# Differential attention: the product of weights and values for two query tiles at a time, in three float32r passes, with its norm and output moved a tile apart

## The chip, the cores and the metric

One core of one Trainium2 chip runs the whole program. The metric is the device time of one execution in microseconds (us). TensorE (PE) multiplies matrices and turns tiles, VectorE (DVE) and ScalarE (ACT) read its results from PSUM, GpSimd (POOL) does small element-wise work, and SyncE (SP) issues the DMAs.

## The reference

The program is a two-layer encoder trunk for 1024 tokens of width 1024. Layer 0 mixes tokens by neighbourhood attention, layer 1 by dense differential attention; each layer ends with a gated convolutional channel mixer and a gated embedding. The change concerns layer 1's mixer: 8 heads, each with two score maps of 64 channels and values of 128 channels.

```python
def diff_attention(h, w_qkv, lam, subln_g, w_o, t5_table, lambda_init):
    ...
    def block_fn(args):            # one block of 128 queries
        ...
        s = jnp.einsum('bhmqd,bhmkd->bhmqk', qb, k).astype(jnp.float32) + bias[None, :, None]
        a = jax.nn.softmax(s, axis=-1)
        w = a[:, :, 0] - lam_full * a[:, :, 1]
        return jnp.einsum('bhqk,bhkd->bhqd', w.astype(v.dtype), v)
    ...
    o = rms_norm(o, subln_g) * (1.0 - lambda_init)
    o = o.transpose(0, 2, 1, 3).reshape(B, S, D)
    return o @ w_o
```

## The kernel before, in words

All matrices are float32. Large products run in float32r, in three passes: an operand is split into a high part (a copy rounded to float32r, `high`, L134, on ACT) and a low part (what the copy left over, `low`, L137, a subtraction on DVE that reads the high part), and `mm3` (L169) adds high x high, high x low and low x high. `split` (L140) is the two together.

The mixer of layer 1 is `da` (L667). It works on chunks: chunk n is one head (n // 8) and one tile of 128 queries (n % 8), 64 chunks in all. For each chunk TensorE does this:

- `da_scores` (L591): both score maps of 128 queries x 1024 keys, 12 matmuls of 64 rows x 512 columns, into four PSUM banks. DVE then adds the bias and finds the row extreme of each map (L441), ACT takes the exponentials and their sums (L445), and DVE combines the two maps to the weights w (L616).
- `da_turn` (L619), twice: half g of the weights, four blocks of 128 x 128, is turned in one bank and copied to `wT`, half 0 by ACT (L631), half 1 by DVE (L633).
- `da_values` (L635): eight plain float32 matmuls, the turned weights as the stationary operand, 128 columns of values moving; the result is query x value. ACT squares and sums it (L645), POOL takes the root (L184), DVE scales (L648). The bank stays in use.
- `da_out` (L651): one transpose of the normed tile into the same bank, then ACT copies it out (L664; L661 in the last head) and SP stores it.

Beside the chunks runs a generator, `qkv_stream`: the projections of queries, keys and values of the next head in 48 steps of three matmuls (L172 to L174), their splits, the weights' loads and splits, and at the end the projected embeddings and the first part of the output product. `tick(part)` (L403) lets it go on by 6 x part steps, carrying fractions over; `need` runs it until a head's operands are there; `drain` runs the rest. The values of the next head are turned through the same two banks (L203) and copied by ACT (L372).

TensorE runs in the order in which the program is written. The order of the other engines is fixed ahead of the run by a planner with a model of times of its own, which in general puts the instruction that is earlier in the program first. Splits of late loads are put in a list of jobs and hung behind the softmax and the half 1 copy of the chunks (`job`, L747).

PSUM has eight banks: four for scores, two for the projections (pool `pj`), two for everything else here (pool `tr`, `bank()`, L126), handed out in turn. The four pages of pool `r2` (16 KB a partition) hold queries and keys of the heads in turn, and afterwards the embedding operands.

Of the kernel before, what the change touches and what calls it, by code (L numbers as in the profile page):

```python
# [8 lines left out]
F32 = mybir.dt.float32  # L9
F32R = mybir.dt.float32r  # L10
AF = mybir.ActivationFunctionType
ALU = mybir.AluOpType
# [4 lines left out]
P = 128  # L17
D = 1024
SEQ = 1024
NT = SEQ // P  # L20
KT = D // P
# [5 lines left out]
D_HEADS = 8  # L27
FT = 22
PK = 2
EPS = 1e-6  # L30
# [61 lines left out]
class Trunk:  # L92
# [88 lines left out]
        return self.root(ss)  # L181

    def root(self, ss):
        self.nc.gpsimd.tensor_tensor(out=ss, in0=ss, in1=self.mhalf, op=ALU.pow)  # L184
        return ss

    def normed(self, x, h, g=None, tag="ss"):
# [30 lines left out]
    def constants(self):  # L218
        nc, c = self.nc, self.const
        self.ident = c.tile([P, P], F32, tag="ident", name="ident")  # L220
        nc.sync.dma_start(self.ident, self.i["c_ident"])

        self.mhalf = c.tile([P, 1], F32, tag="mhalf", name="mhalf")
        nc.vector.memset(self.mhalf, -0.5)

    def late_constants(self):
# [69 lines left out]
    def qkv_stream(self, layer, hT, x, first, mid):  # L296


        nc = self.nc
# [2 lines left out]
        own = [slice(0, 64), slice(64, 128)]  # L302
        values = lambda: None
        for j in range(KT):
            A = self.page(self.r2, "r2", (P, 4, SEQ), F32R)
            if layer == 0:
                B = self.page(self.r2, "r2", (P, 4, SEQ), F32R)
                Q, KH, KL = [A[:, 0], A[:, 1]], [A[:, 2], A[:, 3]], [B[:, 0], B[:, 1]]
# [53 lines left out]
            if layer == 0:  # L362
                v = B[:, 2:4].rearrange("p a (t m w) -> p (a t) m w", t=4, m=2)

                def put(g, t):
                    o, t = v[:, 4 * g : 4 * g + 4], t.rearrange("p k (m w) -> p k m w", m=2)
                    self.split(t, o[:, :, :, 0:64], o[:, :, :, 64:128])
            else:
                v = self.page(x, "v", (P, KT, P))

                def put(g, t):
                    nc.scalar.activation(v[:, 4 * g : 4 * g + 4], t, AF.Copy)  # L372

            vT = self.page(self.raw, "raw")
            for tb in range(2):
# [58 lines left out]
            nc.gpsimd.tensor_tensor(out=v(B), in0=v(self.mask), in1=s, op=ALU.subtract)  # L434
        return B

    def softmax_pre(self, s, bias, e):

        nc = self.nc
        mn = self.col("mn")  # L440
        nc.vector.tensor_tensor_reduce(  # L441
            out=e, in0=s, in1=bias, scale=1.0, scalar=3e38, op0=ALU.add, op1=ALU.min, accum_out=mn
        )
        sm = self.col("sum")
        self.exp = nc.scalar.activation(e, e, AF.Exp, bias=mn, scale=-1.0, accum_out=sm).ins  # L445
        return sm

# [143 lines left out]
    def da_scores(self, x, n):  # L591

        nc = self.nc
        h, t = n // NT, n % NT
        A = self.qk[h]
        if t == 0:
            self.T = self.page(x, "T", (P, TW))
            nc.sync.dma_start(self.T, self.skewed[h][:, P - 1 : P - 1 + TW])
        s = [self.ps.tile([P, 1024], F32, tag="s", name=self.uid("s")) for _ in range(2)]
        q = slice(t * P, t * P + P)  # L600
        for half in range(2):
            w = slice(half * 512, half * 512 + 512)
            for z, (a, b) in enumerate(((0, 2), (0, 3), (1, 2))):
                for m in range(2):
                    o = slice(64 * m, 64 * m + 64)
                    nc.tensor.matmul(s[m][:, w], A[o, a, q], A[o, b, w], start=z == 0, stop=z == 2)  # L606
        a = (NT - 1 - t) * P
        e = [self.page(x, f"E{m}") for m in range(2)]
        r0, sm = [self.softmax_pre(s[m], self.T[:, a : a + SEQ], e[m]) for m in range(2)]
        w = e[0]  # L610
        self.chunk[n] = w, r0
        c = self.col("c")
        nc.vector.reciprocal(c, sm)
        nc.vector.scalar_tensor_tensor(out=c, in0=r0, scalar=c, in1=self.neglam, op0=ALU.mult, op1=ALU.mult)
        nc.vector.reciprocal(r0, r0)
        done = nc.vector.scalar_tensor_tensor(out=w, in0=e[1], scalar=c, in1=w, op0=ALU.mult, op1=ALU.add).ins  # L616
        self.job(self.exp, done)

    def da_turn(self, x, n, g):  # L619
        nc = self.nc  # L620
        w, r0 = self.chunk[n][:2]
        if g == 0:
            self.chunk[n] = w, r0, self.page(x, "wT", (P, KT, P))
        wT = self.chunk[n][2]
        t = self.bank()
        for k in range(4):
            c = (4 * g + k) * P
            nc.tensor.transpose(t[:, k * P : k * P + P], w[:, c : c + P], self.ident)  # L628
        t = t.rearrange("p (k t) -> p k t", k=4)
        if g == 0:  # L630
            self.turned_w = nc.scalar.activation(wT[:, 0:4], t, AF.Copy).ins  # L631
        else:
            self.job(self.turned_w, nc.vector.tensor_copy(wT[:, 4:8], t).ins)  # L633

    def da_values(self, x, n):  # L635
        nc = self.nc
        V = self.v[2 * (n // NT)]
        _, r0, wT = self.chunk[n]
        b = self.bank()
        o = b[:, :P]  # L640
        for k in range(KT):
            nc.tensor.matmul(o, wT[:, k], V[:, k], start=k == 0, stop=k == KT - 1)  # L642
        os = self.page(x, "os", (P, P))
        r = self.col("ss")
        nc.scalar.activation(os, o, AF.Square, scale=r0, accum_out=r)  # L645
        nc.vector.tensor_scalar(out=r, in0=r, scalar1=1.0 / P, scalar2=EPS, op0=ALU.mult, op1=ALU.add)  # L646
        self.root(r)
        nc.vector.tensor_scalar(out=os, in0=o, scalar1=r0, scalar2=r, op0=ALU.mult, op1=ALU.mult)  # L648
        self.chunk[n] = b, os

    def da_out(self, x, n, oT):  # L651
        nc = self.nc
        h, t = n // NT, n % NT
        b, os = self.chunk.pop(n)
        tr = b[:, P : 2 * P]
        nc.tensor.transpose(tr, os, self.ident)
        cols = slice(t * P, t * P + P)
        if h == D_HEADS - 1:
            if t == 0:
                self.opage = self.page(self.raw, "raw")  # L660
            nc.scalar.activation(self.opage[:, cols], tr, AF.Copy, scale=self.subg)  # L661
        else:
            ot = self.page(x, "ot", (P, P))
            nc.scalar.activation(ot, tr, AF.Copy, scale=self.subg)  # L664
            nc.sync.dma_start(oT[h][:, cols], ot)

    def da(self, hT, oT, first, mid):  # L667

        N = NT * D_HEADS
        with self.tc.tile_pool(name="xa1", bufs=2, reuse_waits="tile") as x, \  # L670
             self.psum("s", 2) as self.ps:
            self.begin(self.qkv_stream(1, hT, x, first, mid))
            self.chunk = {}
            self.need(self.qk, 0)
            self.tick(6 / 6)
            self.da_scores(x, 0)
            self.tick(6 / 6)
            for n in range(N + 1):
                if n > 0:
                    self.need(self.v, (n - 1) // NT * 2 + 1)  # L680
                    self.da_values(x, n - 1)
                if n + 1 < N:
                    self.need(self.qk, (n + 1) // NT)
                    self.da_scores(x, n + 1)
                if n < N:
                    self.da_turn(x, n, 0)
                self.tick(0.34)
                if n < N:
                    self.da_turn(x, n, 1)
                self.tick(0.16)  # L690
                if n > 0:
                    self.da_out(x, n - 1, oT)
                self.tick(0.5)
            self.drain()

    def psum(self, name, bufs):
        return self.tc.tile_pool(name=self.uid("ps" + name), bufs=bufs, space=PSUM, reuse_waits="tile")
# [741 lines left out]

    def embeddings(self, layer):  # L1440

        nc = self.nc
        a = self.page(self.r2, "r2", (P, 2, 2, SEQ), F32R)
        b = self.page(self.r2, "r2", (P, 2, 2, D), F32R)
        load = []
        for k in range(2):
            rows = slice(k * P, k * P + P)
            for o, src in ((a, self.i["pT"]), (b, self.i["ple_w_proj"])):
                load.append((src[layer][rows], o[:, k, 0], o[:, k, 1]))
        if layer == 0:  # L1450
            for src, *parts in load:
                self.load_split(src, dst=parts)
        else:
            left = list(load)

            def begin(src, *parts):
                raw = self.page(self.raw, "raw")
                nc.sync.dma_start(raw, src)
                return raw, parts

            next_one = [begin(*left.pop(0))]

            def job():
                raw, parts = next_one.pop()
                did = self.split(raw, *parts)
                if left:
                    next_one.append(begin(*left.pop(0)))
                return did

            self.jobs += [job] * 4  # L1470
        yield
        while layer == 1 and next_one:
# [139 lines left out]
```

## Time and profile before

| | |
|---|---|
| median of 3 runs | 2758.91 us (2757.64 to 2758.96) |
| profiled execution | 2758.85 us, span 2757.1 us |
| PE, PEld (weight loads) | 2693.7 us (98%), 2225.7 us (81%) |
| DVE, ACT, POOL | 1938.5 us (70%), 1321.2 us (48%), 463.2 us (17%) |
| mean granted clock | 0.993 |
| stage of the change | from the first scores at 1348.9 us to the last output near 1928 us |

Busy time counts an instruction from start to end; matmuls overlap, so two starts in a row tell what one costs. The granted clock is given as a share of full speed: 1.00 is 2.4 GHz, 0.50 is 1.2 GHz.

### The profile page before, as it was taken

What the parts mean: (1) busy time and instruction counts of PE and PEld (TensorE: products, weight loads), DVE (VectorE), ACT (ScalarE), POOL (GpSimd) and SP (SyncE); (2) the same over time, 40 slices, a digit from 0 to 9 for tenths busy, and PEclk for the clock granted to TensorE, in tenths of its full rate; (3) what the DMA queues carried; (4) which work ended last, traced back from release to release, by engine and by line L of the source; (5) the groups of instructions that cost most, each with busy time, mean ns of one, the idle gap of its engine ahead of it and who ended that gap; (6) DMA issues with size and microseconds to landing.
All of it is one profiled execution on the core that took longest, in us unless ns stands there. A gap on an engine that the chain in (4) does not pass through costs nothing.

```text
span 2757.1 us, 36537 instructions
## 1 busy us (share of the span) xinstructions
PE 2693.7 (98%) x13440; PEld 2225.7 (81%) x13440; DVE 1938.5 (70%) x3317; ACT 1321.2 (48%) x2467; POOL 463.2 (17%) x461
## 2 busy tenths in 40 slices
PE   7999998999999999999999999999999999999998
PEld 5788887877888888888788888887887888888887
DVE  5677776579777777676566666676688777776664
ACT  4555556454444445454355555555454434444452
POOL 2121220004333310001000000000105333300000
PEclk9999999999999999999999999999999999999999
DMA  6512214533322373343211111123413323272342
GB/s 183 169 55 68 66 48 156 142 92 107 115 102 94 115 263 125 105 150 111 99 46 46 45 46 46 53 77 126 134 62 122 115 92 115 98 284 96 115 146 103
DMA packets 129476, 298.48 MB, mean 108 GB/s; under 512 B 11753, under 2 KB 37737, under 8 KB 129297
## 3 DMA queue, kind: packets, MB, share of 16 engines
q1 hardware_dynamic: 129296, 296.15, 32.5%
q8 instruction: 105, 1.72, 0.3%
q14 instruction: 75, 0.61, 0.1%
HBM read 221.69 MB, written 86.61 MB: 112 GB/s over the span
## 4 chain that ended last, share of the span: by engine, by line
PE 85%; DVE 6%; DMA 4%; ACT 2%; issue 2%; POOL 0%; SPq 0%; ACTq 0%; POOLq 0%; DVEq 0%
PE b L172 19%; PE b L173 19%; PE b L174 19%; PE g L770 6%; PE m L770 5%; PE b L642 4%; PE s L606 3%; PE b L628 2%; PE b L203 2%; PE av L512 1%; PE b L485 1%; DVE r L138 1%; PE b L770 1%; DMA raw<-in_qkv 1%; DMA x<-in_x 1%
## 5 line engine op out<-in xcount | busy, mean ns | idle before, releaser
L172 PE MATMUL b<-r,ws 128*128 128x512 f32 (+1 forms) x1328 | 547.3, 412 | 6.9 <-ACT ws L135 3.7
L173 PE MATMUL b<-r,ws 128*128 128x512 f32 (+1 forms) x1328 | 519.7, 391 | 1.4 <-DVE r L138 1.2
L174 PE MATMUL b<-r,ws 128*128 128x512 f32 (+1 forms) x1328 | 519.1, 391 | 0.5 <-DVE ws L138 0.5
L172 PEld LDWEIGHTS b<-r,ws 128*128 128x128 f32 x1328 | 252.8, 190 | 55.2 <-ACT ws L135 4.1
L174 PEld LDWEIGHTS b<-r,ws 128*128 128x128 f32 x1328 | 252.1, 190 | 54.8 <-DVE ws L138 1.0
L173 PEld LDWEIGHTS b<-r,ws 128*128 128x128 f32 x1328 | 253.3, 191 | 38.6 <-DVE r L138 3.5
L172 PE MATMUL b<-r,r 128*128 128x512 f32 x680 | 270.4, 398 | 9.5 <-ACT r L135 5.2
L184 POOL TENSOR_TENSOR ss<-ss,mhalf 128x1 f32<-128x1 f32 x136 | 84.0, 619 | 1142.1 <-DVE ss L646 563.3
L172 PE MATMUL b<-r,wa 128*128 128x512 f32 x688 | 269.0, 391 | 4.5 <-DVE B L1140 3.7
L445 ACT ACTIVATE E<-E,mn 128x1024 f32<-128x1024 f32 (+2 forms) x256 | 221.4, 866 | 105.2 <-DVE mn L441 104.7
L174 PE MATMUL b<-r,wa 128*128 128x512 f32 x688 | 268.6, 390 | 0.0
L173 PE MATMUL b<-r,wa 128*128 128x512 f32 x688 | 268.4, 390 | 0.0
L174 PE MATMUL b<-r,r 128*128 128x512 f32 x680 | 266.5, 392 | 1.0 <-DVE r L138 1.0
L173 PE MATMUL b<-r,r 128*128 128x512 f32 x680 | 266.8, 392 | 0.5 <-DVE r L138 0.5
L138 DVE TENSOR_TENSOR ws<-raw,ws 128x512 fp32r<-128x512 f32 (+3 forms) x168 | 171.1, 1026 | 61.1 <-ACT ws L135 58.6
L138 DVE TENSOR_TENSOR r<-raw,r 128x512 fp32r<-128x512 f32 (+1 forms) x170 | 129.1, 766 | 113.1 <-ACT r L135 110.0
L135 ACT ACTIVATE r<-raw 128x512 fp32r<-128x512 f32 (+1 forms) x170 | 112.7, 670 | 193.2 <-PE b L173 162.6
L135 ACT ACTIVATE ws<-raw 128x512 fp32r<-128x512 f32 (+3 forms) x168 | 124.3, 748 | 137.4 <-PE b L174 52.1
L172 PEld LDWEIGHTS b<-r,r 128*128 128x128 f32 x680 | 128.6, 189 | 38.6 <-ACT ws L1483 6.3
L770 PE MATMUL m<-r,ws 128*128 128x512 f32 x672 | 156.9, 393 | 0.0
L172 PEld LDWEIGHTS b<-r,wa 128*128 128x128 f32 x688 | 129.4, 188 | 33.5 <-DVE B L1140 5.2
L770 PE MATMUL g<-r,ws 128*128 128x512 f32 x672 | 155.8, 391 | 0.0
(178 smaller groups left out, 5110.4 us busy)
## 6 DMA issues: line engine op xcount, KB each, us to landing
raw<-in_w_in SPq DMA_DIRECT2D x86, 512.0 KB, 3.5
raw<-in_qkv SPq DMA_DIRECT2D x48, 512.0 KB, 5.6
spillS<-r SPq DMA_DIRECT2D x88, 256.0 KB, 3.2
r<-in_ffn_w_out SPq DMA_DIRECT2D x40, 512.0 KB, 10.1
raw<-spillS SPq DMA_DIRECT2D x40, 512.0 KB, 3.5
spillA<-B SPq DMA_DIRECT2D x66, 256.0 KB, 2.9
raw<-spillA SPq DMA_DIRECT2D x30, 512.0 KB, 4.0
x<-x SPq DMA_DIRECT2D x24, 512.0 KB, 3.7
```

Of the source, the lines that this page charges most:

```text
L135: return self.nc.scalar.activation(hi, src, AF.Copy).ins
L138: return self.nc.vector.tensor_tensor(out=lo, in0=src, in1=hi.bitcast(F32), op=ALU.subtract).ins
L172: mm(out, sta[0], mov[0], start=first, stop=False, skip_group_check=onto)
L173: mm(out, sta[0], mov[1], start=False, stop=False, skip_group_check=onto)
L174: mm(out, sta[1], mov[0], start=False, stop=last, skip_group_check=onto)
L184: self.nc.gpsimd.tensor_tensor(out=ss, in0=ss, in1=self.mhalf, op=ALU.pow)
L203: self.nc.tensor.transpose(t[:, k * P : k * P + P], h[:, c : c + P], self.ident)
L445: self.exp = nc.scalar.activation(e, e, AF.Exp, bias=mn, scale=-1.0, accum_out=sm).ins
L606: nc.tensor.matmul(s[m][:, w], A[o, a, q], A[o, b, w], start=z == 0, stop=z == 2)
L628: nc.tensor.transpose(t[:, k * P : k * P + P], w[:, c : c + P], self.ident)
L642: nc.tensor.matmul(o, wT[:, k], V[:, k], start=k == 0, stop=k == KT - 1)
L770: mm(out[half], a, b[:, w], start=first and k + z == 0, stop=last and k == n - 1 and z == 2)
```

## The change

Weights and values are multiplied for two chunks at a time, after the second of them, with the values stationary and 2 x 128 query columns of turned weights moving, in three float32r passes. So the values and the turned weights are split. The result is value x query; ACT copies it to `os`, and it is turned back for the norm (`da_norm`), normed, and turned again for the output (`da_out`). Values, norm and output each take a bank of their own and give it back. In the loop the norm of a pair stands at the end of the even chunk in which its values were made, and its output in the odd chunk after, between the two turns. The turned weights of a pair lie in one page of `r2`; queries and keys use the other three, and the embedding operands two of these, whose second is filled later (`after_keys`). In the diff `mhalf` becomes two columns wide, and `softmax_pre` can put a sum into a given column.

```diff
@@ qkv_stream
-            A = self.page(self.r2, "r2", (P, 4, SEQ), F32R)
+            A = self.page(self.r2, "r2", (P, 4, SEQ), F32R) if layer == 0 else self.pages[j % 3]
...
-                v = self.page(x, "v", (P, KT, P))
+                v = self.page(x, "v", (P, 2, KT, P), F32R)
                 def put(g, t):
-                    nc.scalar.activation(v[:, 4 * g : 4 * g + 4], t, AF.Copy)
+                    self.split(t, v[:, 0, 4 * g : 4 * g + 4], v[:, 1, 4 * g : 4 * g + 4])
@@ da_turn
-        if g == 0:
-            self.turned_w = nc.scalar.activation(wT[:, 0:4], t, AF.Copy).ins
-        else:
-            self.job(self.turned_w, nc.vector.tensor_copy(wT[:, 4:8], t).ins)
+        did = self.split(t.rearrange("p (k t) -> p k t", k=4), *(a[:, 4 * g : 4 * g + 4, u] for a in self.wT))
+        if g == 1:
+            self.job(*did)
@@ da_values
-        o = b[:, :P]
+        o, (hi, lo) = b[:, : 2 * P], self.wT
         for k in range(KT):
-            nc.tensor.matmul(o, wT[:, k], V[:, k], start=k == 0, stop=k == KT - 1)
...
+            self.mm3(
+                o, (V[:, 0, k], V[:, 1, k]), [a[:, k].rearrange("p u t -> p (u t)") for a in (hi, lo)], k == 0, k == KT - 1
+            )
+        os = self.page(x, "os", (P, 2, P), bufs=1)
+        self.nc.scalar.activation(os.rearrange("p u t -> p (u t)"), o, AF.Copy)
+        self.os = os
+
+    def da_norm(self, x, n):
+        nc = self.nc
+        b, os = self.bank().rearrange("p (z u t) -> p z u t", z=2, u=2), self.os
+        r0 = self.sums.pop(0)
+        for u in range(2):
+            nc.tensor.transpose(b[:, 0, u], os[:, u], self.ident)
+        ss = self.page(x, "rms", (P, 2))
+        for u in range(2):
+            nc.scalar.activation(os[:, u], b[:, 0, u], AF.Square, scale=r0[:, u : u + 1], accum_out=ss[:, u : u + 1])
+        nc.vector.tensor_scalar(out=ss, in0=ss, scalar1=1.0 / P, scalar2=EPS, op0=ALU.mult, op1=ALU.add)
+        nc.gpsimd.tensor_tensor(out=ss, in0=ss, in1=self.mhalf, op=ALU.pow)
+        for u in range(2):
+            q, r = (a[:, u : u + 1] for a in (r0, ss))
+            nc.vector.tensor_scalar(out=os[:, u], in0=b[:, 0, u], scalar1=q, scalar2=r, op0=ALU.mult, op1=ALU.mult)
@@ da_out
-        b, os = self.chunk.pop(n)
-        tr = b[:, P : 2 * P]
-        nc.tensor.transpose(tr, os, self.ident)
+        b, os = self.bank().rearrange("p (z u t) -> p z u t", z=2, u=2), self.os
+        for u in range(2):
+            nc.tensor.transpose(b[:, 0, u], os[:, u], self.ident)
...
@@ da
+            self.pages = [self.page(self.r2, "r2", (P, 4, SEQ), F32R) for _ in range(4)]
+            w = self.pages[3].rearrange("p a n -> p (a n)").rearrange("p (z k u t) -> p z k u t", z=2, k=KT, u=2)
+            self.wT = w[:, 0], w[:, 1]
...
-            self.tick(6 / 6)
             self.da_scores(x, 0)
-            self.tick(6 / 6)
+            self.tick(8 / 6)
             for n in range(N + 1):
-                if n > 0:
-                    self.need(self.v, (n - 1) // NT * 2 + 1)
-                    self.da_values(x, n - 1)
                 if n + 1 < N:
                     self.need(self.qk, (n + 1) // NT)
                     self.da_scores(x, n + 1)
+                if n + 1 >= N - NT - 1:
+                    self.jobs += self.after_keys
+                    self.after_keys.clear()
+                if n % 2 == 0 and n > 0:
+                    self.need(self.v, (n - 1) // NT * 2 + 1)
+                    self.da_values(x, n - 1)
                 if n < N:
                     self.da_turn(x, n, 0)
-                self.tick(0.34)
+                    self.tick(0.6)
+                if n % 2 and n > 1:
+                    self.da_out(x, n - 2, oT)
                 if n < N:
                     self.da_turn(x, n, 1)
-                self.tick(0.16)
-                if n > 0:
-                    self.da_out(x, n - 1, oT)
-                self.tick(0.5)
+                    self.tick(0.6 if n % 2 else 0.2)
+                if n % 2 == 0 and n > 0:
+                    self.da_norm(x, n - 1)
             self.drain()
+            self.da_out(x, N - 1, oT)
@@ embeddings
+            a, b = (self.pages[k].rearrange("p (k z) n -> p k z n", k=2) for k in (2, 0))
...
-            self.jobs += [job] * 4
+            self.jobs += [job] * 2
+            self.after_keys += [job] * 2
```

## Rows read from the trace of the kernel before

**Rows 1.** The page, busy us, share of the span and instructions of each engine.
```profile
PE 2693.7 (98%) x13440; PEld 2225.7 (81%) x13440; DVE 1938.5 (70%) x3317; ACT 1321.2 (48%) x2467; POOL 463.2 (17%) x461
```

**Rows 2.** Stretches: length, busy us of PE, PEld, DVE, ACT, POOL, clock, DMA.
```profile
1340.00:1380.00 40.00, 38.78 (x220) 31.13 (x219) 20.96 (x39) 16.58 (x30) 1.09 (x2) 1.00 0.12 42
1500.00:1540.00 40.00, 40.00 (x256) 32.79 (x253) 27.21 (x55) 20.89 (x43) 2.74 (x5) 1.00 0.07 21
1900.00:1940.00 40.00, 34.79 (x178) 28.62 (x177) 18.90 (x36) 14.05 (x32) 3.03 (x6) 0.91 0.37 124
```

**Rows 3.** Waits of TensorE, 1366 to 1935: us in total, times, longest.
```profile
PE b L628 <- ACT wT L631: 3.3, 1, 3.3
PE b L656 <- DVE os L648: 1.9, 1, 1.9
```

**Rows 4.** Timeline of TensorE in one chunk: start, us, instructions.
```profile
1499.70 1.65 PE L606 MATMUL s<-r 64*128 64x512 f32 x12
1501.28 0.65 PE L628 MATMUL b<-ident,E 128*128 128x128 f32 x4
1501.69 0.47 PE L172 MATMUL b<-r,ws 128*128 128x512 f32 x1
1502.00 0.39 PE L173 MATMUL b<-r,ws 128*128 128x512 f32 x1
1502.23 0.40 PE L174 MATMUL b<-r,ws 128*128 128x512 f32 x1
...
1502.92 0.39 PE L174 MATMUL b<-r,ws 128*128 128x512 f32 x1
...
1504.05 0.39 PE L174 MATMUL b<-r,ws 128*128 128x512 f32 x1
1504.29 0.27 PE L656 MATMUL b<-ident,os 128*128 128x128 f32 x1
...
1504.63 0.40 PE L173 MATMUL b<-r,ws 128*128 128x512 f32 x1
...
1506.90 2.01 PE L642 MATMUL b<-v,wT 128*128 128x128 f32 x16
1508.84 1.66 PE L606 MATMUL s<-r 64*128 64x512 f32 x12
```

**Rows 5.** Timeline of TensorE, first and last of 23 matmuls of 256 columns.
```profile
24.63 0.28 PE L173 MATMUL b<-r,ws 128*128 128x256 f32 x1
...
27.26 0.28 PE L174 MATMUL b<-r,ws 128*128 128x256 f32 x1
```

**Rows 6.** Timeline of ACT, DVE and POOL in the next chunk.
```profile
1509.01 0.37 ACT L645 ACTIVATE os<-b,sum 128x128 f32<-128x128 f32 x1 [1.31 <-PE b L642]
...
1509.49 0.15 DVE L646 TENSOR_SCALAR ss<-ss 128x1 f32<-128x1 f32 x1 [2.12 <-ACT os L645]
1509.79 0.55 POOL L184 TENSOR_TENSOR ss<-ss,mhalf 128x1 f32<-128x1 f32 x1 [8.59 <-DVE ss L646]
1510.38 0.41 DVE L648 TENSOR_SCALAR os<-b,sum,ss 128x128 f32<-128x128 f32 x1 [0.73 <-POOL ss L184]
...
1510.70 1.21 DVE L441 CUSTOM_DVE_ANT_0 E<-s,T 128x1024 f32<-128x1024 f32 x1
...
1511.84 1.22 DVE L441 CUSTOM_DVE_ANT_0 E<-s,T 128x1024 f32<-128x1024 f32 x1
...
1512.99 0.69 DVE L633 COPY wT<-b 128x512 f32<-128x512 f32 x1
```

**Rows 7.** Timeline of ACT and DVE, a split of a half elsewhere.
```profile
1331.89 0.60 ACT L135 ACTIVATE r<-b 128x512 fp32r<-128x512 f32 x1 [4.44 <-PE b L203]
...
1332.52 0.69 DVE L138 TENSOR_TENSOR r<-b,r 128x512 fp32r<-128x512 f32 x1 [3.16 <-ACT r L135]
```

**Rows 8.** Groups of instructions, 1366 to 1927: busy us, mean ns, idle before.
```profile
L138 DVE TENSOR_TENSOR ws<-raw,ws 128x1024 fp32r<-128x1024 f32 (+2 forms) x23 | 25.8, 1126 | 0.7 <-ACT ws L135 0.7
...
L138 DVE TENSOR_TENSOR r<-b,r 128x512 fp32r<-128x512 f32 x14 | 9.6, 688 | 0.7
```

More of the change, by code (lines that the diff above doesn't have):

```diff
@@ L183, in root @@
     def root(self, ss):
-        self.nc.gpsimd.tensor_tensor(out=ss, in0=ss, in1=self.mhalf, op=ALU.pow)
+        self.nc.gpsimd.tensor_tensor(out=ss, in0=ss, in1=self.mhalf[:, :1], op=ALU.pow)
         return ss
@@ L221, in constants @@
         nc.sync.dma_start(self.ident, self.i["c_ident"])
-        self.mhalf = c.tile([P, 1], F32, tag="mhalf", name="mhalf")
+        self.mhalf = c.tile([P, 2], F32, tag="mhalf", name="mhalf")
         nc.vector.memset(self.mhalf, -0.5)
@@ L435, in na_bias, with softmax_pre @@
         return B
-    def softmax_pre(self, s, bias, e):
+    def softmax_pre(self, s, bias, e, sm=None):
         nc = self.nc
@@ L443, in softmax_pre @@
         )
-        sm = self.col("sum")
+        sm = self.col("sum") if sm is None else sm
         self.exp = nc.scalar.activation(e, e, AF.Exp, bias=mn, scale=-1.0, accum_out=sm).ins
@@ L608, in da_scores @@
         e = [self.page(x, f"E{m}") for m in range(2)]
-        r0, sm = [self.softmax_pre(s[m], self.T[:, a : a + SEQ], e[m]) for m in range(2)]
-        w = e[0]
-        self.chunk[n] = w, r0
+        if n % 2 == 0:
+            self.sums.append(self.page(x, "r0", (P, 2)))
+        r0 = self.sums[-1][:, n % 2 : n % 2 + 1]
+        bias = self.T[:, a : a + SEQ]
+        self.softmax_pre(s[0], bias, e[0], r0)
+        sm = self.softmax_pre(s[1], bias, e[1])
+        w = self.chunk[n] = e[0]
         c = self.col("c")
@@ L619, in da_turn @@
     def da_turn(self, x, n, g):
-        nc = self.nc
-        w, r0 = self.chunk[n][:2]
-        if g == 0:
-            self.chunk[n] = w, r0, self.page(x, "wT", (P, KT, P))
-        wT = self.chunk[n][2]
+        w, u = self.chunk[n], n % 2
         t = self.bank()
@@ L627, in da_turn @@
             c = (4 * g + k) * P
-            nc.tensor.transpose(t[:, k * P : k * P + P], w[:, c : c + P], self.ident)
-        t = t.rearrange("p (k t) -> p k t", k=4)
-        if g == 0:
-            self.turned_w = nc.scalar.activation(wT[:, 0:4], t, AF.Copy).ins
-        else:
-            self.job(self.turned_w, nc.vector.tensor_copy(wT[:, 4:8], t).ins)
-    def da_values(self, x, n):
-        nc = self.nc
-        V = self.v[2 * (n // NT)]
-        _, r0, wT = self.chunk[n]
-        b = self.bank()
-        o = b[:, :P]
-        for k in range(KT):
-            nc.tensor.matmul(o, wT[:, k], V[:, k], start=k == 0, stop=k == KT - 1)
[L643 to L649, printed above, removed]
+            self.nc.tensor.transpose(t[:, k * P : k * P + P], w[:, c : c + P], self.ident)
@@ new lines, in da_turn @@
+        did = self.split(t.rearrange("p (k t) -> p k t", k=4), *(a[:, 4 * g : 4 * g + 4, u] for a in self.wT))
+        if g == 1:
+            self.job(*did)
+    def da_values(self, x, n):
+        V = self.v[2 * (n // NT)]
+        b = self.bank()
+        o, (hi, lo) = b[:, : 2 * P], self.wT
+        for k in range(KT):
+            self.mm3(
[4 more added lines that the diff above has]
+        self.os = os
@@ L651, in da_out @@
     def da_out(self, x, n, oT):
         nc = self.nc
-        h, t = n // NT, n % NT
-        b, os = self.chunk.pop(n)
-        tr = b[:, P : 2 * P]
-        nc.tensor.transpose(tr, os, self.ident)
-        cols = slice(t * P, t * P + P)
+        h, t = n // NT, n % NT - 1
+        b, os = self.bank().rearrange("p (z u t) -> p z u t", z=2, u=2), self.os
+        for u in range(2):
+            nc.tensor.transpose(b[:, 0, u], os[:, u], self.ident)
+        cols = slice(t * P, t * P + 2 * P)
         if h == D_HEADS - 1:
@@ L660, in da_out @@
                 self.opage = self.page(self.raw, "raw")
-            nc.scalar.activation(self.opage[:, cols], tr, AF.Copy, scale=self.subg)
+            out = self.opage[:, cols]
         else:
-            ot = self.page(x, "ot", (P, P))
-            nc.scalar.activation(ot, tr, AF.Copy, scale=self.subg)
-            nc.sync.dma_start(oT[h][:, cols], ot)
+            out = self.page(x, "ot", (P, 2 * P), bufs=1)
+        nc.scalar.activation(out, b[:, 0].rearrange("p u t -> p (u t)"), AF.Copy, scale=self.subg)
+        if h < D_HEADS - 1:
+            nc.sync.dma_start(oT[h][:, cols], out)
     def da(self, hT, oT, first, mid):
@@ L671, in da @@
              self.psum("s", 2) as self.ps:
+            self.pages = [self.page(self.r2, "r2", (P, 4, SEQ), F32R) for _ in range(4)]
+            w = self.pages[3].rearrange("p a n -> p (a n)").rearrange("p (z k u t) -> p z k u t", z=2, k=KT, u=2)
+            self.wT = w[:, 0], w[:, 1]
             self.begin(self.qkv_stream(1, hT, x, first, mid))
-            self.chunk = {}
+            self.chunk, self.sums, self.after_keys = {}, [], []
             self.need(self.qk, 0)
-            self.tick(6 / 6)
             self.da_scores(x, 0)
-            self.tick(6 / 6)
+            self.tick(8 / 6)
             for n in range(N + 1):
-                if n > 0:
-                    self.need(self.v, (n - 1) // NT * 2 + 1)
-                    self.da_values(x, n - 1)
                 if n + 1 < N:
@@ L1442, in embeddings @@
         nc = self.nc
-        a = self.page(self.r2, "r2", (P, 2, 2, SEQ), F32R)
-        b = self.page(self.r2, "r2", (P, 2, 2, D), F32R)
+        if layer == 0:
+            a, b = (self.page(self.r2, "r2", (P, 2, 2, D), F32R) for _ in range(2))
+        else:
+            a, b = (self.pages[k].rearrange("p (k z) n -> p k z n", k=2) for k in (2, 0))
         load = []
-        for k in range(2):
-            rows = slice(k * P, k * P + P)
-            for o, src in ((a, self.i["pT"]), (b, self.i["ple_w_proj"])):
+        for o, src in ((a, self.i["pT"]), (b, self.i["ple_w_proj"])):
+            for k in range(2):
+                rows = slice(k * P, k * P + P)
                 load.append((src[layer][rows], o[:, k, 0], o[:, k, 1]))
```

## The prediction, written before the change was timed

> **What bounds the kernel now.** I read the engine totals first: TensorE has work in flight in 98% of the span, the vector engine (DVE) 70%, the scalar engine (ACT) 48% [rows 1]. That is a mean over stages, so the table of stretches comes next. In the attention stage of layer 1 a stretch of 40 us has TensorE in flight for all 40.00 us at full clock, DVE busy 27.21 us and ACT 20.89 us [rows 2]. The waits of TensorE over the whole stage (1366 to 1935 us) say the same: the two longest are single events of 3.3 and 1.9 us, both in the last 30 us [rows 3], and the three groups below them add 1.6 us. So in this stage time is the sum of what TensorE issues; DVE and ACT run in its shadow, one query tile ahead. A change that issues less there gains all of it, until it makes TensorE wait.
>
> **What TensorE issues.** From the timeline of one query tile [rows 4]. Values: 16 records (two for each of 8 float32 matmuls) from 1506.90 to 1508.84, 1.94 us. Scores: from 1499.70 to the first transpose at 1501.28, 1.58 us. One projection step (three matmuls): 1502.23 to 1502.92, 0.69 us, so 0.23 a matmul. Four transposes: 1501.28 to 1501.69, and the next matmul then takes 0.31 instead of 0.23, so 0.49 in all. The single transpose of the output: two matmul intervals with it take 0.58 (1504.05 to 1504.63) instead of 0.46, so 0.12.
>
> After: for two tiles together, 8 x 3 matmuls of 256 columns in float32r instead of 2 x 16 records. That form runs at the start of this kernel, with a weight load each: 22 intervals from 24.63 to 27.26 us, 0.1195 us each [rows 5]. 24 x 0.1195 = 2.87 us against 2 x 1.94 = 3.88: 1.01 less a pair, 32.3 us over 32 pairs. I take this row because size, type and clock are the same; at the 0.23 of a 512-column matmul, which is the ceiling, the 24 would cost 5.5 us, 1.6 more than before.
>
> The result now lies as value x query, so it is turned twice: two transposes in the norm and two in the output for each pair, where before there was one a tile. A transpose in a group costs 0.49/4 = 0.12, so 4 x 0.12 = 0.49 instead of 2 x 0.12 = 0.25: +0.24 a pair, +7.8 us. Projection steps, scores and weight transposes are unchanged in number (6 + 6 steps a pair became 3.6 + 1.2 + 3.6 + 3.6). So TensorE issues 32.3 - 7.8 = 24.5 us less.
>
> **What the other engines get.** Each half of a tile's transposed weights was one copy, half 0 on ACT, half 1 on DVE (0.69 us, [rows 6]). Now each half is a split: a copy on ACT, then on DVE a subtraction that reads the copy, 0.60 and then 0.69 us, the second starting when the first is done (1331.89, 1332.52) [rows 7]. A pair has four: DVE +2 x 0.69, ACT +2 x 0.60. The values are split too (two DVE operations more a head, 0.35 a pair), and one small DVE operation of the two goes. A pair took about 18.3 us, and DVE was 68% busy, 12.4 us [rows 2]; 12.4 + 1.4 + 0.35 - 0.15 = 14.0 us in 17.5 is 80%. ACT goes from 52% (9.6 us a pair) to some 63% (two split copies more; the copy of the values' result and one long output copy for two short ones). Neither becomes the bound by its sum. Edits that I cost at nothing: output DMAs halve in number and double in width, and only the output copy of the next pair, 17 us later, waits for them, so SP is relieved; GpSimd takes two columns in one operation instead of one in each of two; queries and keys go round three pages instead of four, and a page is written again when its head's scores ended two heads before. If that last cover failed, TensorE would stand for microseconds at each head, plain in the waits.
>
> **The new wait.** Two banks serve the stage's transposes, values, norm and output in turn. On an even tile the order is values, half 0, half 1, norm; on an odd one half 0, output, half 1. So half 1 of an odd tile takes the bank of its own half 0, and must wait until that half's subtraction on DVE has ended. Before, the second half waited for an ACT copy (half 0) alone, and ACT was free then.
>
> I count from S, the start of the scores on an odd tile. TensorE is ready for half 1 at S + 1.58 (scores) + 0.49 (half 0) + 4 x 0.69 (the tick of 0.6 is 3.6 steps and finds 0.8 carried over) + 0.24 (output) = S + 5.07. DVE must first do what comes earlier in the program and is ready: the two score reductions (1.14 apart, the one behind at 1.15: 1510.70, 1511.84, 1512.99), the two norm operations of the pair before (0.32 apart, 1510.38 to 1510.70) [rows 6], then the subtraction. Scores end at S + 1.66 [rows 4]. If the first reduction goes first: 1.66 + 1.14 + 0.64 + 1.15 + 0.69 = S + 5.28, a wait of 0.21, 0.27 with a release. If the norm goes first, its chain decides: transposes end near S + 0.2, two squares of 0.46 (ACT to DVE took 0.48, 1509.01 to 1509.49), then 0.30 to GpSimd and 0.59 back [rows 6]: S + 2.03 for the first norm operation, so reductions from S + 2.67 and the subtraction ends at S + 5.65: a wait of 0.6. I take the middle, 0.45: 32 x 0.45 = 14.4 us. Ends: 0, if the subtraction is put ahead of the second reduction (it then ends near S + 4.2; what that puts back by 0.7, the softmax of the next tile, is due a whole tile later); 0.6, or 19 us.
>
> On top come the projection's own DVE operations. Per head: three weight subtractions of 1.13, four of 0.69 for queries and keys [rows 8], two for the values: 7.5 us. They can stand ahead of the awaited subtraction in about 4.6 of a pair's 17.5 us: 2.0 us a head, 16 us at most, nothing if all fall elsewhere. I take a third, 5.3 us, because DVE still idles a fifth of the time.
>
> **Ends of the stage.** The last output waited 1.9 us for the norm [rows 3]. Now the loop's last pass has no tick (six steps before), so about five projection steps are left for the drain, and stand between the last norm and the last output: they cover its chain of 2 to 3 us. A new wait of about 0.6 us comes between the last values and the norm's transposes (the copy on ACT). I count -1. The 3.3 us wait came from ACT's queue, blocked by a copy ahead; the jobs are ordered anew there (two of the embedding splits now wait for head 6's page), and both kinds of half now need ACT. I count it unchanged, with -5 and +5 as ends: gone with its clock dip, or doubled.
>
> **Sum.** -24.5 + 14.4 + 5.3 - 1 = -5.8 us. The profiled execution took 2758.85 us (span 2757.1 and 1.75 around it), 0.06 below the median of the runs, 2758.91. Forecast 2753 us.
>
> **Rivals.**
>
> A, no new wait: the order on DVE lets the subtractions through. For it: the softmax has slack, DVE is at 80%. Against it: the reduction is earlier in the program and ready earlier. Gain 24.5 + 1: 2733 us.
>
> B, DVE's queue takes the gain and more: in the odd tiles the awaited subtraction stands behind both reductions, the norm and a projection operation in most pairs. It decides from a mean wait of (24.5 + 1)/32 = 0.8 us a pair. At 1.15 (0.6 and half of a weight subtraction) the waits are 36.8 us: 2758.85 - 25.5 + 36.8 = 2770. For it: nine projection operations a head to collide with, and a second wait like it at the norm when the values' transposes shift the order of the two banks. Against it: DVE idled 2.1 and 0.7 us around the norm of a single tile [rows 6].
>
> C, the clock falls. It was 0.91 of full speed over the stretch with the 3.3 and 1.9 us waits [rows 2]: 0.09 x 40 = 3.6 us lost in two dips from 2.4 to 1.2 GHz, 1.8 each. The stretch from 1340 to 1380, with 1.2 us of waits (40.00 - 38.78), stayed at 1.00. Regular waits could do what one long one did. A dip in each fourth pair would put 8 x 1.8 = 14 us on my sum: 2767. A dip in every pair would put 32 x 1.8 = 58 us on it: 2811. For it: the waits come once in 17.5 us through the whole stage. Against it: each is well under the 1.2 us that left the clock alone. The Trainium skill (TensorE: Matmul & The Clock Gate, section on a second failure mode, cycling through PSUM banks) describes this case: frequent short idles of TensorE between groups, made by going round the banks, let the clock swing between its levels. By that rule the time would be the 2811, an estimate; the stretch that idled 1.2 us at full clock speaks against it.
>
> The Trainium skill's advice on bubbles (Trainium Kernel Development and Optimization, Best Practices) is that regular ones can mean that PSUM ran out. Before, no regular wait shows [rows 3], so by the trace two banks were enough; with the change I expect exactly such a regular bubble.
>
> **How the numbers follow.** My own case, waits of 0.3 to 0.75 us a pair with the tail's ends, 53%: 2743 to 2762 (-25.5 + 9.6, and -25.5 + 24 + 5). A 21%, B 18%, C 8% (2% of it the large form). About 0.2% (5.5 us) is what a measurement of this kernel can tell from no change: faster is below 2753.4, slower above 2764.4. My case lies half on either side of the first bound: 24% faster, 27% same, 2% slower. A adds 21% to faster; B is 4% same and 14% slower; C 1% same and 7% slower. Faster 0.45, same 0.32, slower 0.23. Range 2733 to 2769: it holds my case, most of A and the first half of B and C.
>
> **What would show it.** Matmul row of the values: 768 records instead of 1024, about 120 ns apart; if further, the first term fails. Waits of TensorE: a group of some 32 on the weight transposes, released by DVE's subtraction, 0.3 to 0.75 us each; none is A, over 0.8 is B. In the timeline of an odd tile: on DVE two reductions and two norm operations between half 0 and its subtraction. DVE near 32 of 40 us. Clock 1.00 in the stretches between 1400 and 1850; below is C. Wrong altogether if scores wait for the softmax, or values for the weights.

## The result, and the profile after

The changed kernel takes 2771.87 us (median of 5 runs, 2768.29 to 2773.01), the kernel before 2758.96 on the same chip (2757.64 to 2760.32). The ratio is 1.0043, with an interval of 1.0031 to 1.0054: slower by some 13 us. Forecast were 2753, and a range that ended at 2769. The profiled execution took 2771.87 us with a span of 2770.1, 13.0 more than before.

The first row of the page, to be set beside [rows 1]:

```profile
PE 2688.0 (97%) x13248; PEld 2206.4 (80%) x13248; DVE 1980.4 (71%) x3365; ACT 1352.6 (49%) x2531; POOL 451.4 (16%) x429
```

TensorE has 192 matmul records fewer and is busy 5.7 us less, while the span is 13.0 longer: its work shrank and it now stands. The totals alone would have hidden that, 97% looks like 98%. The stretches of the kernel after (columns as in [rows 2]):

```profile
1340.00:1380.00 40.00, 38.17 (x205) 29.91 (x203) 24.76 (x44) 19.65 (x32) 0.00 (x0) 0.96 0.13 40
1380.00:1420.00 40.00, 38.90 (x237) 30.94 (x236) 30.41 (x58) 22.09 (x47) 2.09 (x3) 1.00 0.17 58
1500.00:1540.00 40.00, 39.12 (x239) 31.49 (x238) 29.98 (x57) 22.58 (x48) 1.38 (x2) 1.00 0.06 20
1860.00:1900.00 40.00, 35.18 (x215) 27.52 (x214) 31.05 (x54) 29.12 (x56) 1.38 (x2) 1.00 0.36 134
1900.00:1940.00 40.00, 32.68 (x181) 26.20 (x180) 22.42 (x42) 21.54 (x47) 1.82 (x3) 0.91 0.40 136
```

From 1500 to 1540 TensorE was busy 40.00 of 40 us; now it is 39.12. From 1860 to 1900 the kernel before had 39.60, now 35.18. The waits of TensorE from 1360 to 1950 (engine, line and what it waited for: us in total, times, longest) name the cause:

```profile
PE b L629 <- DVE r L138: 14.0, 23, 1.3
PE b L791 <- ACT ws L1508: 4.8, 1, 4.8
PE b L653 <- DVE r L138: 4.7, 8, 2.3
PE b L174 <- DVE v L138: 1.5, 1, 1.5
```

L629 are the transposes of the weights, released by L138, the subtraction of a split on DVE: the group that the forecast asked for. L653 are the norm's transposes, with the same releaser. Before, none of the two groups was there [rows 3].

One odd tile shows the wait. Timeline of the kernel after (start, us, instruction, idle before it and its releaser), S = 1523.20:

```profile
1523.20 1.65 PE L606 MATMUL s<-r 64*128 64x512 f32 x12
...
1524.23 0.17 DVE L657 TENSOR_SCALAR rms<-rms 128x2 f32<-128x2 f32 x1 [0.52 <-ACT os L656]
...
1524.78 0.66 PE L629 MATMUL b<-ident,E 128*128 128x128 f32 x4
...
1525.27 0.73 DVE L661 TENSOR_SCALAR os<-b,r,rms 128x128 f32<-128x128 f32 x2 [0.87 <-POOL rms L658]
...
1525.48 0.60 ACT L135 ACTIVATE r<-b 128x512 fp32r<-128x512 f32 x1 [1.28 <-PE b L629]
...
1525.91 1.22 DVE L441 CUSTOM_DVE_ANT_0 E<-s,T 128x1024 f32<-128x1024 f32 x1
...
1527.05 1.22 DVE L441 CUSTOM_DVE_ANT_0 E<-s,T 128x1024 f32<-128x1024 f32 x1
...
1528.03 0.38 PE L668 MATMUL b<-ident,os 128*128 128x128 f32 x2
...
1528.19 0.69 DVE L138 TENSOR_TENSOR r<-b,r 128x512 fp32r<-128x512 f32 x1
...
1528.94 0.65 PE L629 MATMUL b<-ident,E 128*128 128x128 f32 x4 [0.53 <-DVE r L138]
```

Half 0 is copied by ACT by S + 2.9. Its subtraction has its input then, but stands on DVE behind the norm (S + 2.07) and two score reductions (S + 2.71, S + 3.85), and ends at S + 5.68. Half 1 begins at S + 5.74, 0.91 us after the output's transposes, where it follows them by 0.22 if nothing holds it (the second experiment): 0.69 late. The idle time printed (0.53) is less, because the modelled end of the matmul ahead covers part of it; starts against starts give the true figure. From here on a time per pair is such a figure, the mean over the 24 pairs from the scores of tile 4 to those of tile 52. The kernel before took 17.565 us a pair, the kernel after 17.895. (The 18.3 us a pair in the prediction is twice one tile in which values were turned too; the sum does not use it.)

### The profile page after: what moved, and what is told of

Same layout as the page of the kernel before. It is cut to its first block, busy times and chain, and to the rows that moved or that the text cites. A ratio compares the mean times of both kernels' runs of the same rounds, so it can differ in the third digit from the quotient of the medians.

```text
span 2770.1 us, 35945 instructions
## 1 busy us (share of the span) xinstructions
PE 2688.0 (97%) x13248; PEld 2206.4 (80%) x13248; DVE 1980.4 (71%) x3365; ACT 1352.6 (49%) x2531; POOL 451.4 (16%) x429
## 4 chain that ended last, share of the span: by engine, by line
PE 79%; DVE 10%; DMA 4%; ACT 3%; issue 2%; POOL 1%; SPq 0%; ACTq 0%; POOLq 0%; DVEq 0%
PE b L172 19%; PE b L173 19%; PE b L174 19%; PE g L791 6%; PE m L791 5%; DVE r L138 2%; DVE E L441 2%; PE b L629 2%; PE s L606 2%; PE b L203 2%; PE av L512 1%; PE b L485 1%; PE b L791 1%; DMA raw<-in_qkv 1%; DMA x<-in_x 1%
## 5 line engine op out<-in xcount | busy, mean ns | idle before, releaser
L138 DVE TENSOR_TENSOR ws<-raw,ws 128x512 fp32r<-128x512 f32 (+3 forms) x168 | 169.2, 1014 | 59.0 <-ACT ws L135 57.4
L138 DVE TENSOR_TENSOR r<-raw,r 128x512 fp32r<-128x512 f32 (+1 forms) x170 | 129.3, 768 | 111.7 <-ACT r L135 108.5
L135 ACT ACTIVATE r<-b 128x512 fp32r<-128x512 f32 x208 | 121.0, 593 | 107.4 <-PE b L629 87.6
L138 DVE TENSOR_TENSOR r<-b,r 128x512 fp32r<-128x512 f32 x208 | 140.8, 686 | 39.1 <-ACT r L135 38.8
L441 DVE CUSTOM_DVE_ANT_0 E<-s,T 128x1024 f32<-128x1024 f32 x128 | 151.8, 1221 | 18.3 <-PE s L606 18.2
```

The source lines that it names most:

```text
L135: return self.nc.scalar.activation(hi, src, AF.Copy).ins
L138: return self.nc.vector.tensor_tensor(out=lo, in0=src, in1=hi.bitcast(F32), op=ALU.subtract).ins
L441: nc.vector.tensor_tensor_reduce(out=e, in0=s, in1=bias, scale=1.0, scalar=3e38, op0=ALU.add, op1=ALU.min, accum_out=mn)
```

## The experiments

Theory: TensorE's gain is real, but smaller than forecast, and odd tiles give it back at the bank of half 0. Rivals: the gain is not there at all (the values cost what they did); or DVE's load, not its order, is what costs; or the time is lost at the stage's end alone.

**Another use of the bank's time.** The output is turned after half 1 instead of before it, so that half 1 gets the other bank:

```
                 if n < N:
                     self.da_turn(x, n, 0)
                     self.tick(0.6)
-                if n % 2 and n > 1:
-                    self.da_out(x, n - 2, oT)
                 if n < N:
                     self.da_turn(x, n, 1)
-                    self.tick(0.6 if n % 2 else 0.2)
+                    self.tick(0.3 if n % 2 else 0.2)
+                if n % 2:
+                    if n > 1:
+                        self.da_out(x, n - 2, oT)
+                    self.tick(0.3)
```

> The changed kernel with one move: on an odd tile the output's transposes stand after half 1 instead of before it, so half 1 takes the bank of the norm and not that of its own half 0. Theory (the wait is for the bank, held until DVE's subtraction of half 0): the 0.62 us a pair between output and half 1 go, 20 us in 32 pairs, from 2771.9 to about 2752 us. Rival (DVE's in-order queue is late as a whole, and the bank is only where it shows): the wait comes back at the values or at the next tile's weights, time 2765 us or more.

Measured: 2748.5 us, ratio to before 0.9964 (0.9951 to 0.9976), 23 us less than the change. The group of L629 shrank to one event:

```profile
PE b L653 <- DVE r L138: 4.1, 7, 2.4
...
PE b L629 <- DVE r L138: 0.3, 1, 0.3
```

A pair takes 17.296 us, 0.60 less. So the change's gain is there, and the bank's order gave it away.

**Another order on DVE, the bank as it was.** The second score reduction is written after the turning of half 0, and held behind that half's subtraction on odd tiles:

```
         self.softmax_pre(s[0], bias, e[0], r0)
-        sm = self.softmax_pre(s[1], bias, e[1])
+        self.rest = n, s[1], bias, e, r0
...
+    def da_weights(self):
...
+        sm = self.softmax_pre(s1, bias, e[1])
+        if n > 0 and n % 2 == 0:
+            self.behind((self.min,), self.last_half)
...
                     self.da_turn(x, n, 0)
+                if n + 1 < N:
+                    self.da_weights()
```

> The changed kernel with one order edge on DVE: the second score reduction of the next tile comes after the subtraction of half 0 on odd tiles; banks and TensorE's order are as in the changed kernel. Theory (the order of four DVE operations ahead of the subtraction makes the wait): the subtraction ends near S + 4.5 instead of 5.7, TensorE is ready at 5.07, the wait goes, about 2752 us. Rival (DVE lacks the capacity): the second reduction, 0.7 later, makes the softmax late instead and the next tile's weights wait, 2765 us or more.

Measured: 2746.11 us, 0.9952 (0.9939 to 0.9964). Timeline of the same odd tile as above, S = 1514.66; here L636 is the turning of the weights, L676 that of the output:

```profile
1514.66 1.65 PE L606 MATMUL s<-r 64*128 64x512 f32 x12
...
1516.73 0.73 DVE L669 TENSOR_SCALAR os<-b,r,rms 128x128 f32<-128x128 f32 x2 [0.87 <-POOL rms L666]
...
1517.37 1.21 DVE L441 CUSTOM_DVE_ANT_0 E<-s,T 128x1024 f32<-128x1024 f32 x1
...
1518.51 0.68 DVE L138 TENSOR_TENSOR r<-b,r 128x512 fp32r<-128x512 f32 x1
...
1519.11 1.21 DVE L441 CUSTOM_DVE_ANT_0 E<-s,T 128x1024 f32<-128x1024 f32 x1
...
1519.51 0.38 PE L676 MATMUL b<-ident,os 128*128 128x128 f32 x2
1519.72 0.60 PE L636 MATMUL b<-ident,E 128*128 128x128 f32 x4
```

The same DVE operations, two of them exchanged: the subtraction ends at S + 4.53, as expected, and half 1 starts 0.22 after the output, in every one of the 24 pairs. The wait that the rival asked for, for the next tile's weights, did not come: the stage has one of 0.2 us. It is the order, then, not DVE's load: DVE does the same work (1981.7 us busy in the whole program, 1980.4 in the change) and a pair falls from 17.895 to 17.242. This run and the one before came out 5.9 and 3.5 us under the 2752 expected. Of its 25.8 us under the change, 0.653 x 32 = 20.9 are the steady pairs'; the rest lies at the stage's ends.

**Later by a step.** The ticks of odd tiles 0.8 and 0.4 instead of 0.6 and 0.6, so that 1.2 projection steps more on average, 0.8 us, stand between half 0 and half 1:

```
-                    self.tick(0.6)
+                    self.tick(0.8 if n % 2 else 0.6)
...
-                    self.tick(0.6 if n % 2 else 0.2)
+                    self.tick(0.4 if n % 2 else 0.2)
```

> The changed kernel with one projection step moved on odd tiles from behind half 1 to ahead of the output (ticks 0.8 and 0.4 instead of 0.6 and 0.6). Theory: TensorE comes 0.69 later to half 1, so waits of 0.71, 0.89, 0.71 and 0.19 in four pairs become 0.02, 0.20, 0.02 and 0, about 0.06 a pair; nothing else moves, so about 2754 us. Rival (the cost is TensorE's own issue, transposes and changes of operand kind, and the waits are only where it is late): time stays within 3 us of 2771.9.

Measured: 2754.33 us, 0.9982 (0.9973 to 0.9991), about as expected, but not by quite the expected route. The bank's wait was covered in three pairs of four; in the fourth a new one came, 1.15 us by the starts, since the projection's turning of the values moved with the ticks and its subtraction now stands ahead. A pair takes 17.478 us, 0.417 less than the change, where about 0.56 was expected; that the time still came out at 2754 is in part luck at the ends. The waits of the new kind:

```profile
PE b L629 <- DVE v L138: 6.1, 7, 1.0
```

**The stage's end alone.** One ACT copy of the output product is held behind the last half's split:

```
                 second = self.out_part(layer, order[1])
+                if layer == 1:
+                    self.behind(self.did, self.last_half)
```

> The changed kernel with one order edge at the end of the stage: the first split of the output projection that waits for a page stands on ACT behind the last weight split instead of ahead of two softmax steps. Theory: the single wait of 4.8 us there and its clock dip of about 1.8 us go, 2771.9 to about 2765 us. Rival: the embedding result's page is late for TensorE in any case and the time moves by under 2 us.

What it takes away is this, in the kernel after: a copy at the head of ACT's queue waits for a DMA, the copy at L1508 waits behind it, and TensorE for that:

```profile
1921.37 0.95 ACT L135 ACTIVATE ws<-raw 128x896 fp32r<-128x896 f32 x1 [2.57 <-DMA pp<-ws]
...
1923.83 0.58 ACT L1508 ACTIVATE ws<-b 128x512 f32<-128x512 f32 x1
...
1924.47 0.80 PE L791 MATMUL b<-r,ws 128*128 128x512 f32 x1 [4.76 <-ACT ws L1508]
```

Measured: 2763.93 us, 1.0017 (1.0008 to 1.0026): 7.9 less than the change, as expected, and still slower than before. A pair takes 17.894 us, as in the change. Its waits and its last stretch:

```profile
PE b L629 <- DVE r L138: 14.1, 24, 1.3
...
PE b L792 <- ACT ws L1511: 1.2, 1, 1.2
```

```profile
1900.00:1940.00 40.00, 36.58 (x207) 29.57 (x206) 24.04 (x46) 21.26 (x48) 2.62 (x4) 1.00 0.53 178
```

The wait of 4.8 became 1.2, which is 3.6 us, and the clock stayed at 1.00 where it had been 0.91 over 40 us, another 3.6 (twice the dip that was expected). The end alone does not explain the loss.

**Both together**: the order on DVE and the end.

> The two order edges together: the second score reduction behind the subtraction of half 0 on odd tiles, and the output projection's first split behind the last weight split. Theory (two separate waits, one steady on DVE, one at the end on ACT): they add up, and the 3.3 and 1.6 us that are left at the end go down to about 1.2: 2746.1 - 4 = about 2742 us, faster than both kernels. Rival (with the steady wait gone the end is bound by DVE, not by ACT): within 1.5 us of 2746.

Measured: 2743.12 us, 0.9943 (0.9931 to 0.9956), a pair 17.239. With the end mended the order is worth 20.8 us (2763.93 to 2743.12), without it 25.8; the end is worth 7.9 without the order and 3.0 with it, so the two overlap by about 5 us. This run and the two below were measured beside a kernel before of 2757.72 us, those above beside one of 2758.72, so 1.0 of the 3.0 may be that difference. What was expected at the end did not come: the wait of 3.3 us became 2.0 and that of 1.6 stayed. The theory's 2742 and the rival's 2744.5 or more lie too close together for this run to decide between them.

**The wait that is left, at the norm.** Its place in the kernel after, once a head, is behind the turning of the values (L203):

```profile
1504.30 0.60 PE L203 MATMUL b<-ident,raw 128*128 128x128 f32 x4
1505.18 0.44 PE L653 MATMUL b<-ident,os 128*128 128x128 f32 x2 [0.28 <-DVE r L138]
```

The values' turning takes a bank in between, the order of the two shifts, and the norm gets the bank of a half that DVE has not left yet. It starts 0.88 us after L203, where a successor that waits for nothing starts 0.35 after it. To the version with both edges one edit is added, which turns the first half of those values two projection steps earlier:

```
-                    if tb == 1 and kt == (4, 7)[layer]:
+                    if tb == 1 and kt == (4, 5)[layer]:
```

> As the run with both order edges, and the first four blocks of a head's values are turned two projection steps earlier. In the changed kernel they stand directly ahead of a norm and shift the two banks, so that once a head the norm waits 0.53 us for half 1's subtraction. Theory: that wait goes, 7 heads x 0.53 = about 4 us: 2738 us. Rival: the turned values now take the bank between the halves and half 1 of an even tile waits instead: no gain or up to 4 us slower.

Measured: 2742.07 us, 0.9940 (0.9927 to 0.9952). The group is gone but for one long event, which the version with both edges has too (2.4) and which now has another releaser; the rival's wait at half 1 did not come (one of 0.2 us at L636):

```profile
PE b L661 <- DVE v L138: 2.3, 1, 2.3
```

A pair takes 17.084 us, 0.155 less, which is 3.7 us in the 24 pairs; but the run gained 1.05 in the median, which the intervals do not tell from nothing. In the profiled runs its first scores stand 2.0 us later (1344.41 against 1342.38), so some of the gain was lost ahead of the first tile; in the other profiled runs built on the change that start lies anywhere from 1342.38 to 1345.41, so it may be no more than the scatter of single runs. What the edit is worth in the whole is not shown. It is the fastest complete version here, 0.6% under the kernel before and 29.8 us under the change.

**The price of a values matmul.** On the version with order and end, with one of three passes left out:

```
         for k in range(KT):
-            self.mm3(
-                o, (V[:, 0, k], V[:, 1, k]), [a[:, k].rearrange("p u t -> p (u t)") for a in (hi, lo)], k == 0, k == KT - 1
-            )
+            h = hi[:, k].rearrange("p u t -> p (u t)")
+            for z in range(2):
+                self.nc.tensor.matmul(o, V[:, z, k], h, start=k + z == 0, stop=k == KT - 1 and z == 1)
```

> As the run with both order edges, with one of the three passes of the values left out (values high x weights low), so 16 matmuls a pair instead of 24; all else is kept. It prices a matmul of the values by itself. Theory: 8 x 0.12 = 0.96 us a pair, 31 us in 32 pairs, so 2742 - 31 = 2711 us. Rival (weight loads or DVE, not the columns, set the pace of the values): a gain of less than 20 us.

Measured: 2724.14 us, 0.9874 (0.9859 to 0.9889), 19.0 less, not 31: in time the rival's case. But the values' own price held: 2.979 us a pair for 24 matmuls and 2.017 for 16, so 0.96 for 8, 0.12 for each with its weight load (which of the two sets the 0.12, this run cannot tell). The loss is elsewhere, and DVE makes it: a pair fell by 0.626 only (17.239 to 16.613). TensorE now comes so early that in one pair of four half 0 of an odd tile finds its bank, that of the half 1 before, still in use: it starts 2.41 us after the scores instead of 1.59, because two subtractions of the projection (1475.31, and one of 0.68 behind it) stand on DVE ahead of the awaited one. That is 0.20 of the 0.33 lost a pair; the rest are shorter waits.

```profile
1475.31 1.22 DVE L138 TENSOR_TENSOR ws<-raw,ws 128x1024 fp32r<-128x1024 f32 x1
...
1475.37 1.65 PE L606 MATMUL s<-r 64*128 64x512 f32 x12
...
1477.04 0.68 DVE L138 TENSOR_TENSOR r<-b,r 128x512 fp32r<-128x512 f32 x1
...
1477.78 0.44 PE L636 MATMUL b<-ident,E 128*128 128x128 f32 x2 [0.75 <-DVE r L138]
```

The waits of this kind in the whole stage:

```profile
PE b L636 <- DVE r L138: 9.0, 14, 1.9
```

Two stretches of 1500 to 1540 us, the version it is built on and then this one:

```profile
1500.00:1540.00 40.00, 40.00 (x247) 32.39 (x246) 30.21 (x60) 23.18 (x47) 1.38 (x2) 1.00 0.05 17
```

```profile
1500.00:1540.00 40.00, 39.70 (x243) 31.72 (x242) 31.49 (x61) 23.91 (x51) 1.38 (x2) 1.00 0.06 14
```

With the order mended TensorE is in flight for all of the 40.00 us again; take a third of the values away, and it waits for an engine that is busy 31.49 of 40 us. This further cut on TensorE was worth about two thirds of its length.

## Why the prediction was wrong

**The step that failed** is the first term, what TensorE issues less: 24.5 us forecast, about 14.6 measured. With the order mended a pair takes 17.242 us, of which 0.13 is the norm's wait that is left, against 17.565 before, so TensorE issues about 0.455 less a pair, times 32. The mechanism is right, its size is not, in both halves.

The values before were priced by one row, 1.94 us, and that row [rows 4] is one of the six highest of 48, one a head; other values were being turned right ahead of it (L203, 1506.46). The next tiles of the kernel before:

```profile
1515.63 1.95 PE L642 MATMUL b<-v,wT 128*128 128x128 f32 x16
1517.50 1.66 PE L606 MATMUL s<-r 64*128 64x512 f32 x12
...
1524.30 1.95 PE L642 MATMUL b<-v,wT 128*128 128x128 f32 x16
1526.17 1.66 PE L606 MATMUL s<-r 64*128 64x512 f32 x12
```

From the start of the values to that of the scores it is 1.87 us, and the mean of 48 is 1.883: 3.766 a pair, not 3.88. After, the 24 matmuls do stand 0.12 apart, but for one:

```profile
1533.18 0.39 PE L172 MATMUL b<-r,v 128*128 128x256 f32 x1
1533.40 0.28 PE L173 MATMUL b<-r,v 128*128 128x256 f32 x1
1533.52 0.28 PE L174 MATMUL b<-r,v 128*128 128x256 f32 x1
...
1536.04 0.28 PE L174 MATMUL b<-r,v 128*128 128x256 f32 x1
...
1536.16 0.60 PE L629 MATMUL b<-ident,E 128*128 128x128 f32 x4
```

The first, behind the scores, takes 0.22. The rows at the kernel's start [rows 5] begin one matmul too late to show this: the matmul of 256 columns ahead of them, the first behind transposes, takes 0.20 to the next start (24.63):

```profile
24.43 0.36 PE L172 MATMUL b<-r,ws 128*128 128x256 f32 x1
```

The 24 come to 2.975, and the saving is 3.766 - 2.975 = 0.79 a pair instead of 1.01: 7.0 us of the miss, half from the one row and half from the first matmul.

The transposes cost +0.33 a pair (all that a pair takes beside the values: 14.13 with the order mended, the norm's wait of 0.13 taken off, against 13.80 before) instead of +0.24: 2.9 us. The two pairs of transposes take 0.33 (ahead of the scores) and 0.22 (ahead of half 1) to the next start, 0.54 where 0.49 was counted. Starts summed by line over the 24 pairs show the rest: the single transposes before took 0.05 themselves, and the projection's matmuls and the weights' transposes are now 0.21 shorter, together 0.26 where 0.25 was counted; scores and the turning of the values (without the norm's wait) are 0.04 longer, which was not counted.

**The new wait** was right in place and form, and nearly so in its total. Where the norm goes first the subtraction was to end at S + 5.65; it ends at S + 5.68, and half 1 starts at S + 5.74 in 11 of the 24 pairs (at 5.67 in one), at S + 5.87 to 5.93 in 6. In the other 6 a reduction goes first, and the subtraction ends at S + 5.30, where 5.28 was forecast. The waits in excess of 0.217 us come to 0.60 a pair, and the transposes behind a wait take 0.06 more in all: 21.1 us over 32 pairs, against 14.4 + 5.3 = 19.7. That the total fits so well is in part luck. The norm goes first in 18 of 24 pairs, so the middle (0.45) was too low; and the 5.3 us for projection operations ahead of the awaited subtraction came by another way: none stands between the copy of half 0 and that subtraction. In 6 pairs one delays the norm by 0.2 us, and in the 6 where a reduction goes first it is one that holds the norm back, which makes the wait shorter, 0.18.

**A wait not in the sum**: the norm's, 0.53 once a head (0.13 a pair, 4.2 us if counted over 32 pairs like the other terms). The prediction named it only as a point for rival B.

**The ends** came to +2.3 instead of -1, which is what is left of 13.0 (-14.6 + 21.1 + 4.2 + 2.3). The 3.3 us wait of ACT's queue became 4.8 [rows 3], behind the same copy that waits for a DMA and within the bounds given, and in the last tiles half 1 started up to 1.71 us after the output.

The misses are 9.9, 1.4, 4.2 and 3.3 us, together the 18.8 between -5.8 and +13.0. So the result came out as rival B gave it (2770), from another cause: the waits did not grow to 1.15 a pair, they are 0.8 with the norm's, but the gain they had to outweigh was 0.46 a pair and not 0.8.

**Rival A**, no new wait, is what the runs with order or bank changed show, at 2746 and 2748.5 us and not at its 2733, since the gain is smaller than forecast. **Rival C** is out in the steady part: each of the twelve stretches from 1380 to 1860 has the clock at 1.00, with a wait of 0.2 to 0.9 us in every pair. The rule of the Trainium skill (TensorE: Matmul & The Clock Gate, on a second failure mode, cycling through PSUM banks) says that such frequent idles make the clock swing; these stretches do not bear it out. The clock did fall in the stretch from 1340 to 1380 (0.96, with one wait of 1.5) and in that from 1900 to 1940 (0.91, with one of 4.8). But a long wait did not always bring it down: the stretch from 1860 to 1900 holds one of 2.3 (L653) and stands at 1.00, and the run with the stage's end alone has the same wait of 1.5 between 1340 and 1380 and keeps 1.00 there:

```profile
1340.00:1380.00 40.00, 38.17 (x219) 29.44 (x218) 25.87 (x48) 20.96 (x37) 0.70 (x1) 1.00 0.11 38
```

By the rule's 2811 us an engineer would have mended the clock, when the order on DVE was what had to be mended.

The other rule of the Trainium skill (Trainium Kernel Development and Optimization, Best Practices, on consistent bubbles) the trace bears out: regular waits came, and PSUM's two banks were what ran out. Another bank was not tried; a changed order did it with the two.

## What to carry to other kernels

A saving of many small instructions is priced by the mean of all of them, start against start, and by what stands ahead of the first, before waits of the same size are set against it. When a bank's release moves to an engine with a queue, ask what stands ahead of the releasing instruction and whether that is due later: exchanging two DVE instructions was worth 21 to 26 us here, more than the 14.6 that the change saves on TensorE. Once it is mended, look for the next engine: a third off the values gave two thirds of its length, the rest went into waits, most of them for DVE.

## What was not expected of the hardware

The first 256-column matmul behind the 64-row scores takes 0.22 us, all that follow 0.12. Waits of 0.2 to 0.9 us, once in each 17.9 us, left the clock at 1.00 from 1380 to 1860. One wait of 1.5 us was followed by a fall of the clock in the kernel after and not in the run with the stage's end alone. The printed idle time before a matmul is short of the delay between starts (0.53 against 0.69), so a list of waits adds up to less than what is lost: 14.0 us are printed at L629, 0.60 x 32 = 19.3 are lost by the starts.
